# Expert weights of a mixture layer in 2 MB transfers of 16 KB rows, into pairs of slots

## Chip, cores, metric

One core of a Trainium2 chip runs the whole kernel. The metric is device time in microseconds (us) of one launch, lower is better.

## What is computed

One layer over 256 latent tokens and 256 context tokens of width 1024: a conditioned norm, one input projection, two attention branches (8 query heads over 2 key heads; 8 heads through low-rank projections), their gated sum, an output projection and a gated residual; then a second conditioned norm and a mixture of 32 experts, of which each token uses 4:

```python
x = x + g1 * y
x = x + g2 * _moe(_modulate(x, p['norm_ffn'], sh2, sc2), p)
# _moe, for each expert and its tokens xb:
gu = xb @ p['expert_w1'][eid] + p['expert_b1'][eid]      # 1024 x 2048
x_glu = jnp.minimum(gu[..., :1024], 7.0)
x_lin = jnp.clip(gu[..., 1024:], -7.0, 7.0)
act = x_glu * jax.nn.sigmoid(1.702 * x_glu) * (x_lin + 1)
y = act @ p['expert_w2'][eid] + p['expert_b2'][eid]      # 1024 x 1024
```

All of it is float32. The experts' weights are 32 x 12 MB, 384 MB (1 MB is 1,048,576 bytes; GB/s count 10^9 bytes).

## The kernel before

**The front** (the norm, projections, attention, output projection) is cut into named steps, generators whose every `yield` ends a piece. `PLAN`, a list of names written out at the top, says in which order the pieces are emitted (`mixer`); a step that needs another finishes that one first (`needs`). Weights of the front come through three buffers `w` of 1 MB, loaded by SyncE, which issues nearly all transfers, in one order. Products of the front split each operand into two float32r parts and multiply three times (`mm3`, L172 to L174). `reload` (step "x") folds the second norm's scale into the router weights `rw`; `out_chunk` adds the output projection to x, transposes x by 128 columns (`transpose`, L190) and multiplies by `rw` to get the router logits.

**The experts' weights** travel in 384 parts of 1 MB, 12 per expert: part i < 8 holds rows 128 i to 128 i + 127 of w1 (one 8 KB row per partition), parts 8 to 11 hold 256 rows of w2, two neighbouring rows (8 KB) per partition. `expert_part` takes the next slot of `RING`, 20 slots of 1 MB in fixed order (z0 z1, e0 to e3, n0 to n3, m0 m1, g0 g1, three w, y0 y1, r0), and issues the transfer (L105). A slot is a tile, so the transfer waits on SyncE until the readers of what lay there are done. Most slots serve the attention first. `ahead_of_time` fetches parts before the expert loop, by steps of the plan: EZ fetches 2 (z), EA 8 (e, n, when the attention's pools close), EG 4 (m, g). The other six slots come when the loop starts.

**Routing** (`route`) normalises x into `xn`, picks four experts per token, and numbers the tokens of each expert; an expert's first 64 tokens take part in the loop, and `overflow` handles the rest (it is skipped at run time where there are none).

**The expert loop** (`experts`, in an order kept by `keep_order`): for each pair of experts `gather` (L988) multiplies one-hot matrices with `xn` (xn is the loaded operand, 128 x 128) to fetch the tokens, transposed, and applies the second norm's scale and shift per column (`A2`, `B2`, eight columns of 128 features). `up` (L1013 biases, L1020 weights) accumulates 8 parts of w1. `swiglu` runs on VectorE and ScalarE. `turned` transposes the activations (L190, four transposes, every second element of a row of 256). `down` (L1054) accumulates 4 parts of w2, and `scatter` (L1069, L1070) adds the weighted rows to x. TensorE works on the gather of the next pair, or the scatter of the last, while `swiglu` runs. An expert with an even number scatters the pair before it, an odd one gathers for the next pair. Expert 2 also adds the second biases (`bias2`, L969).

Which feature lies in which partition is set by the slices of x and xn (128 features in a row) and by w1's rows; for w2 by `turned`.

Of the kernel before, what the change touches and what calls it, by code (L numbers as in the profile page):

```python
# [6 lines left out]
F32 = mybir.dt.float32  # L7
# [18 lines left out]
l3 h2 l4 k4 r4 r7 c0 EZ k5 c1 f7 k6 l2 h6 end T1 q0*4 q1 kv*2 ss q0 kv r6 q0 q1 kv q1*2 h5 l7 q1 q0 q1*2 g0 q0  # L26
kv q0 EZ mp rest*2 q1*2 q0 T1 g0 q0 g0 c7 g0 g1 c5 g0 c3 q1 g1 q1 g0*3 mp g1*2 g2 kv h7 S0 g2 EZ l6 P0 g0 g1*2
rest g2 g1*2 S2 mp P1 g2*3 g3 rest g2 g3 rest g1 rest S1 c4 S2 P2 l5 end g2 S0 rest S4 S6 rest V3 V2 S4 S3 P3
g3 rest g3*2 S5 S3 c6 g3*2 g2 P4 a0 g3 rest*2 a0 S6 g3 a0 rest a0*2 P5 rest*2 S5 rest V1 rest g2 S7 P6 rest*3
g3 S7 V6 a1 rest b0 k7 rest V0 a1*3 P7 S8 rest*2 a1 rest a0 V8 rest b1 V7 b1 b0 S1 b0 rest a2 P9 b0 V5 a0*2  # L30
rest a2 a1 a2*2 a1 b0 S10*2 V9 V4 a2 a3 b1 rest wa0 b0 b2 S8 V11 a3*4 a1 P13 a1 wa0 a3 a2*2 wa0 S12 rest*2 wa0
S12 rest b1 wa0 P8 wa0 b1 rest wa0 b2 P12 S11 S13 wa0 wa1 rest S9 S15 a3 P10 b2 wa1 wa0 a2 wa1 S9 a2 a3 S13
wa1*3 b3 a0 wa1 S11 b3 V12 V13 b2 S14*2 EA a3 wa1 wb0 b3 EA wb0 b2 P11 wb0 EA S15 wa1 wb0*3 rest wb0 EA wa1
wa0 wb1 b3 wb0*2 wb1 P14 b2 EA wb1 o0 late o0 wb1 rest wb1 o0 P15 wb1 late wb1 EA o0 wb1 o0*2 b1 o0 EA wb1
o1*2 wb1 late o0 o1*2 o0 EG*2 o1 o0*2 rest o1 V14 EG*2 V15 wb0 wb1 late wb0 o0 wb0 o1 late x EG V10 rest o1 b3
o1 EA wb1 late*3 EA b3 o1*3
"""
SLOTS = ("e0", "e1", "e2", "e3", "m0", "m1", "g0", "g1", "y0", "y1", "z0", "z1")
LATER = ("n0", "n1", "n2", "n3")

RING = ("z0", "z1", "e0", "e1", "e2", "e3") + LATER + ("m0", "m1", "g0", "g1") + ("w",) * NW + ("y0", "y1", "r0")

# [4 lines left out]

R_GQ, R_GK, R_MQ, R_MK, R_RB, R_N = 0, 128, 256, 448, 640, 672


class Layer:
# [9 lines left out]
    def open(self, ctx, name, bufs, **kw):  # L61
        self.n += 1
        kw.setdefault("reuse_waits", "tile")
        if name in ("ws", "r"):
            kw["side"] = "right"
        self.pools[name] = ctx.enter_context(self.tc.tile_pool(name=f"{name}{self.n}", bufs=bufs, **kw))
# [9 lines left out]
    def s(self, slot, shape, dt=F32):  # L76

        return self.tile("k" if slot == "x" else "s", shape, dt, slot, 1)

# [12 lines left out]

    def wx(self, shape, dt=F32):
        slot = RING[self.nx % len(RING)]
        self.nx += 1
        if slot == "w":
            return self.w(shape, dt)
        return self.tile({"n": "q", "r": "r"}.get(slot[0], "s"), shape, dt, slot, 1)
# [12 lines left out]
    def ahead_of_time(self, n):  # L111
        for _ in range(n):
            self.ahead.append(self.expert_part())
            yield

    def after_attention(self):
        self.attention.close()
        self.open(self.ctx, "q", 1)
        for slot in LATER:
            self.q([128, 2, D], slot, 1)  # L120
        self.q([128, D], "xg", 1)
        yield from self.ahead_of_time(8)

# [666 lines left out]
    def out_chunk(self, c):  # L790
# [7 lines left out]
        for t in range(2):  # L798
# [33 lines left out]
    def mixer(self):  # L832
# [7 lines left out]
        def gates(c):  # L840
            if c // 2 not in self.ga:
# [132 lines left out]
    def gather(self, e0):  # L974
# [139 lines left out]
    def overflow(self):  # L1114
# [6 lines left out]
        with tc.If(rv > 64):  # L1121
# [12 lines left out]
            with tc.For_i(0, NE, 1) as i:  # L1134
# [80 lines left out]
def pack(inputs):  # L1215
# [72 lines left out]
```

## Time and profile before

| | |
|---|---|
| median of 3 runs | 1319.28 us (1316.31 to 1319.49) |
| the profiled execution | 1318.76 us |
| its span, first to last instruction | 1317.0 us |
| mean granted TensorE clock in it | 0.978 |
| PE busy | 1220.3 us, 93% |
| weights' transfers (hardware queue) | 466.30 MB (10^6 bytes), 87.3% of 16 engines |
| expert transfers | 384 of 1 MB |

Times in rows are us from the first instruction, "x8" counts instructions, and L1020 is line 1020 of the kernel above. PE is TensorE's products, PEld its loading of the stationary operand, SPq SyncE's issuing of transfers. In rows of the chain a piece "DMA r<-in_w_dram" lasts from issue to landing.

### The profile page before, as it was taken

The page shows a single profiled execution, that of the slowest core. Times are in us where ns is not written, and L with a number is a line of the kernel's source. Part 1 is how long each engine was busy: PE and PEld are TensorE (multiplying, and loading weights), DVE is VectorE, ACT ScalarE, POOL GpSimd, SP SyncE. Part 2 cuts the span into 40 slices and gives each one's busy share as a digit, 9 for nine tenths or more (in the row PEclk, how much of TensorE's full clock was granted, in tenths as well). Part 3 has the DMA queues.
Part 4 walks back from the last instruction along what each step waited for, and adds up shares of the span by engine and source line. Part 5 has one row for each costly group of instructions (what it writes and reads, how often), then busy time and mean ns, then how long its engine had stood idle before and what let it go on. Part 6 is the DMA issues. An engine that isn't in the chain of part 4 may idle for free.

```text
span 1317.0 us, 15464 instructions
## 1 busy us (share of the span) xinstructions
PE 1220.3 (93%) x6143; PEld 594.7 (45%) x6143; DVE 475.4 (36%) x1037; ACT 289.3 (22%) x624; POOL 36.8 (3%) x84
## 2 busy tenths in 40 slices
PE   6999999899979999999999999999898998989896
PEld 4777776678744343333334333333323233333332
DVE  5578679876531312122221213222121221212122
ACT  2376778665420000001100001000000010000000
POOL 0220001000000000000000000000000000000000
PEclk8999999999989999999999999999999999999999
DMA  9834462258889999999999999999999999999995
GB/s 346 316 144 168 171 230 87 99 180 329 325 344 409 414 373 405 419 420 419 420 420 420 419 419 419 420 421 419 419 420 420 420 419 420 420 419 420 420 419 206
DMA packets 67324, 467.34 MB, mean 355 GB/s; under 512 B 7632, under 2 KB 8016, under 8 KB 11952
## 3 DMA queue, kind: packets, MB, share of 16 engines
q1 hardware_dynamic: 67248, 466.30, 87.3%
q8 instruction: 50, 0.82, 0.3%
q14 instruction: 26, 0.21, 0.0%
HBM read 465.23 MB, written 1.05 MB: 354 GB/s over the span
## 4 chain that ended last, share of the span: by engine, by line
PE 65%; DMA 27%; DVE 5%; ACT 2%; issue 1%; SPq 0%; POOL 0%; DVEq 0%; ACTq 0%; POOLq 0%
PE bs L1020 21%; PE bx L1054 11%; DMA r<-in_w_dram 8%; DMA m<-in_w_dram 6%; DMA n<-in_w_dram 5%; DMA e<-in_w_dram 5%; PE bacc L172 3%; PE bacc L173 3%; PE bacc L174 3%; DMA w<-in_w_dram 3%; PE bacc L988 2%; PE bx L277 2%; PE bx L190 2%; PE bacc L1069 2%; PE bt L988 2%; PE bt L1069 2%
## 5 line engine op out<-in xcount | busy, mean ns | idle before, releaser
L1028 DVE TENSOR_SCALAR a<-bs 128x512 f32<-128x512 f32 x32 | 22.1, 692 | 435.9 <-PE bs L1020 435.9
L1029 ACT ACTIVATE a<-a 128x512 f32<-128x512 f32 x32 | 20.1, 630 | 716.0 <-DVE a L1028 716.0
L1060 DVE TENSOR_TENSOR y<-bx,g 64x512 f32<-64x512 f32 x64 | 44.1, 689 | 212.3 <-PE bx L1054 211.6
L1020 PE MATMUL bs<-e,xg 128*64 128x512 f32 x416 | 94.2, 595 | 4.1 <-DMA e<-in_w_dram 4.1
L1020 PE MATMUL bs<-n,xg 128*64 128x512 f32 x400 | 90.8, 595 | 3.5 <-DMA n<-in_w_dram 3.5
L139 DVE TENSOR_TENSOR wl<-w,wh 128x512 fp32r<-128x512 f32 (+1 forms) x108 | 74.6, 696 | 30.1 <-ACT wh L138 29.4
L988 PE MATMUL bacc<-c,xn 128*128 128x128 f32 x256 | 42.1, 331 | 38.8 <-DVE c L981 38.8
L1020 PE MATMUL bs<-w,xg 128*64 128x512 f32 x312 | 72.2, 597 | 5.0 <-DMA w<-in_w_dram 4.9
L138 ACT CAST wh<-w 128x512 fp32r<-128x512 f32 (+1 forms) x108 | 65.4, 611 | 44.9 <-PE bacc L174 33.3
L988 PEld LDWEIGHTS bacc<-c,xn 128*128 128x128 f32 x256 | 38.3, 236 | 52.3 <-DVE c L981 51.0
L1020 PEld LDWEIGHTS bs<-e,xg 128*64 128x64 f32 x416 | 28.9, 137 | 67.1 <-issue 57.0
L1020 PEld LDWEIGHTS bs<-n,xg 128*64 128x64 f32 x400 | 27.7, 137 | 64.3 <-issue 56.4
L1020 PE MATMUL bs<-g,xg 128*64 128x512 f32 x208 | 47.7, 597 | 2.2 <-DMA g<-in_w_dram 2.2
L1054 PE MATMUL bx<-n,a 128*64 128x512 f32 x208 | 48.9, 613 | 0.7 <-ACT a L1042 0.7
L1020 PE MATMUL bs<-y,xg 128*64 128x512 f32 x208 | 47.4, 594 | 2.2 <-DMA y<-in_w_dram 2.2
L1020 PE MATMUL bs<-z,xg 128*64 128x512 f32 x208 | 47.5, 596 | 1.1 <-DMA z<-in_w_dram 1.1
L1054 PE MATMUL bx<-e,a 128*64 128x512 f32 x208 | 47.1, 595 | 0.0
L1020 PE MATMUL bs<-m,xg 128*64 128x512 f32 x192 | 44.0, 595 | 2.1 <-DMA m<-in_w_dram 2.1
L1020 PEld LDWEIGHTS bs<-w,xg 128*64 128x64 f32 x312 | 21.1, 136 | 53.9 <-issue 40.8
L998 POOL TENSOR_TENSOR c<-c,gm 128x128 f32<-128x128 f32 x32 | 12.1, 401 | 978.4 <-DVE c L981 854.8
L988 PE MATMUL bt<-c,xn 128*128 128x128 f32 x256 | 37.7, 296 | 0.0
L988 PEld LDWEIGHTS bt<-c,xn 128*128 128x128 f32 x256 | 35.5, 215 | 0.0
(360 smaller groups left out, 1949.8 us busy)
## 6 DMA issues: line engine op xcount, KB each, us to landing
e<-in_w_dram SPq DMA_DIRECT2D x78, 1024.0 KB, 19.9
n<-in_w_dram SPq DMA_DIRECT2D x76, 1024.0 KB, 19.9
w<-in_w_dram SPq DMA_DIRECT2D x57, 1024.0 KB, 19.9
z<-in_w_dram SPq DMA_DIRECT2D x40, 1024.0 KB, 19.9
m<-in_w_dram SPq DMA_DIRECT2D x38, 1024.0 KB, 19.9
g<-in_w_dram SPq DMA_DIRECT2D x38, 1024.0 KB, 19.9
y<-in_w_dram SPq DMA_DIRECT2D x38, 1024.0 KB, 19.9
w<-in_ada_dram SPq DMA_DIRECT2D x24, 1024.0 KB, 6.6
```

Of the source, the lines that this page charges most:

```text
L138: self.nc.scalar.copy(h, src)
L139: self.nc.vector.tensor_sub(l, src, h.bitcast(F32))
L172: mm(o, lh, rh, start=start, stop=False, **kw)
L173: mm(o, lh, rl, start=False, stop=False, **kw)
L174: mm(o, ll, rh, start=False, stop=stop, **kw)
L190: self.nc.tensor.transpose(o, i, self.ident)
L277: nc.tensor.matmul(b[j:j + 32, :256], c, u[:, kk], start=kk < 4, stop=kk >= 4, tile_position=(0, j))
L988: nc.tensor.matmul(b[:, kk % 2], self.xn[:, t, kk * 128:(kk + 1) * 128], oh[:, t], start=t == 0, stop=t == 1)
L1020: mm(b[64 * j:64 * j + 64], xg[:, k, e % 2], w[:, lo:lo + 512], start=False, stop=k == 7, tile_position=(0, 64 * j))
L1054: nc.tensor.matmul(b[64 * j:64 * j + 64], lh, w[:, i, j * 512:(j + 1) * 512], start=f == 0, stop=f == 7, tile_position=(0, 64 * j))
L1060: nc.vector.tensor_mul(y[r:r + 64, cs], b[q], self.g2[q, cs])
L1069: nc.tensor.matmul(b, G[r, t * 128:(t + 1) * 128], y[r, cs], start=True, stop=True)
```

## The change

**Transfers.** `RING` becomes nine pairs of slots (Z E F N O G M W Y, 2 MB each) and two single slots (V R), 20 MB as before. A transfer into a pair fetches two parts: of w1 256 rows, two neighbouring rows (16 KB) per partition; of w2 512 rows, four neighbouring rows (16 KB) per partition. `weights` hands out the halves one after the other. Single transfers of 1 MB fetch one half of such a unit (8 KB out of each 16 KB): in V and R, for parts 20 and 21, and for the last four parts. Pairs are persistent tiles, so a pair's transfer waits for both halves' readers.

**Order of features.** With two rows of w1 per partition, block k of 128 features holds every second feature of a group of 256. `rows(a, k)` takes these columns with step 2: in `gather`, in `out_chunk`'s transposes and in `normed_T` (overflow). The second norm's gains, shift and scale weights and the router weights are permuted alike on the host, in `pack`. `turned` transposes with step 4, and `down` takes one row block per part of `weights`.

**Space and plan.** e0 to e3 move to a pool of the attention; m, y and w buffers to pools that close before routing, behind which M, Y, W, V and R open. Ahead of the loop EZ fetches one pair, EA four (E F N O), EG one (G). `PLAN` is another list.

```diff
 PLAN = """
-f0 h0 f1 T0 bi T0 h1 T0 l0 l1 k0 f2 r1 T1 k1 r2 r0 c2 r3 T0*2 f3 k2 h3 f4 k3 T0 T1*2 h4 T1 T0 tab T1 r5 f5 f6
...
+r0 f0 h0 f1 T0 bi T0 h1 l1 k0 T0 l0 f2 T1 k1 c2 r3 T0*2 f3 k2 h3 f4 k3 h4 T1 tab r5 l3 r1 f6 h2 T0 f5 k4 r7 T1
...
 """
-RING = ("z0", "z1", "e0", "e1", "e2", "e3") + LATER + ("m0", "m1", "g0", "g1") + ("w",) * NW + ("y0", "y1", "r0")
+RING = "ZEFNOGMWYVR"
+def rows(a, k):
+
+    return a[:, k // 2 * 256 + k % 2:k // 2 * 256 + 256:2]
...
     def expert_part(self):
         e, i = divmod(self.nx, 12)
-        src = self.I["w1"][e, i * 128:i * 128 + 128] if i < 8 else self.I["w2"][e, i * 256 - 2048:i * 256 - 1792]
-        w = self.wx([128, 2 * D] if i < 8 else [128, 2, D])
-        self.nc.sync.dma_start(w, src if i < 8 else src.rearrange("(p j) d -> p j d", j=2))
-        return w
+        at = self.nx % sum(1 if slot in "VR" else 2 for slot in RING)
+        slot = "VR"[at - 18] if at >= 18 else RING[at // 2]
+        o = i % 2
+
+        size = 1 if slot in "VR" or 20 <= self.nx < 22 or self.nx >= 12 * NE - 4 else 2
+        self.nx += size
+        lo = 0 if slot in "VR" else at % 2 * 2 * D
+        ap = self.slots[slot][:, lo:lo + size * 2 * D]
+        if i < 8:
+            u = i // 2 * 256
+            src = self.I["w1"][e, u:u + 256].rearrange("(p j) f -> p j f", j=2)[:, o:o + size]
+            dst = ap.rearrange("p (j f) -> p j f", j=size)
+        else:
+            u = (i - 8) // 2 * 512
+            src = self.I["w2"][e, u:u + 512].rearrange("(p j) d -> p j d", j=4)[:, 2 * o:2 * o + 2 * size]
+            dst = ap.rearrange("p (j d) -> p j d", j=2 * size)
+        self.nc.sync.dma_start(dst, src)
+        return [dst[:, j] for j in range(dst.shape[1])]
     def weights(self):
-        return self.ahead.pop(0) if self.ahead else self.expert_part()
+        if not self.ahead:
+            self.ahead += self.expert_part()
+        return self.ahead.pop(0)
...
-                self.transpose(b[:, j], self.x[:, t, c * 512 + j * 128:c * 512 + (j + 1) * 128])
+                self.transpose(b[:, j], rows(self.x[:, t], 4 * c + j))
...
-        w.update(EZ=self.ahead_of_time(2), EA=self.after_attention(), EG=self.ahead_of_time(4))
+        w.update(EZ=self.ahead_of_time(1), EA=self.after_attention(), EG=self.ahead_of_time(1))
...
-                nc.tensor.matmul(b[:, kk % 2], self.xn[:, t, kk * 128:(kk + 1) * 128], oh[:, t], start=t == 0, stop=t == 1)
+                nc.tensor.matmul(b[:, kk % 2], rows(self.xn[:, t], kk), oh[:, t], start=t == 0, stop=t == 1)
...
-        pairs = act.rearrange("q (u p i) -> q u i p", u=2, i=2)
-        for c in range(4):
-            self.transpose(b[:, c], pairs[:, c // 2, c % 2])
+        rows = act.rearrange("q (p i) -> q i p", i=4)
+        for i in range(4):
+            self.transpose(b[:, i], rows[:, i])
...
-        for u in range(4):
+        for f in range(8):
             w = self.weights()
-            for i in range(2):
-                f = 2 * u + i
-                lh = aT[:, f % 4, u // 2 * 64:u // 2 * 64 + 64]
-                for j in range(2):
-                    nc.tensor.matmul(b[64 * j:64 * j + 64], lh, w[:, i, j * 512:(j + 1) * 512], start=f == 0, stop=f == 7,
-                                     tile_position=(0, 64 * j))
+            lh = aT[:, f % 4, f // 4 * 64:f // 4 * 64 + 64]
+            for j in range(2):
+                nc.tensor.matmul(b[64 * j:64 * j + 64], lh, w[:, j * 512:(j + 1) * 512], start=f == 0, stop=f == 7,
+                                 tile_position=(0, 64 * j))
...
+        for slot in "MYW":
+            self.slots[slot] = self.tile("r", [128, 4 * D], F32, slot, 1)
+        self.slots["V"] = self.tile("r", [128, 2 * D], F32, "V", 1)
+        self.slots["R"] = self.tile("r", [128, 2 * D], F32, "R", 1)
```

## Rows read from the trace of the kernel before

**Rows 1.** The page: span, slices of clock, DMA and rate, the chain's shares.
```profile
span 1317.0 us, 15464 instructions
...
PEclk8999999999989999999999999999999999999999
DMA  9834462258889999999999999999999999999995
GB/s 346 316 144 168 171 230 87 99 180 329 325 344 409 414 373 405 419 420 419 420 420 420 419 419 419 420 421 419 419 420 420 420 419 420 420 419 420 420 419 206
...
PE 65%; DMA 27%; DVE 5%; ACT 2%; issue 1%; SPq 0%; POOL 0%; DVEq 0%; ACTq 0%; POOLq 0%
```

**Rows 2.** Windows: length, busy PE PEld DVE ACT POOL (instructions), PEclk, DMA share, GB/s.
```profile
350.00:380.00 30.00, 26.17 (x167) 19.03 (x167) 15.07 (x52) 9.84 (x23) 0.76 (x2) 0.89 0.73 270
...
460.00:470.00 10.00, 10.00 (x44) 2.83 (x44) 2.64 (x4) 0.00 (x0) 0.00 (x0) 0.85 0.71 262
...
490.00:496.00 6.00, 6.00 (x37) 3.26 (x37) 0.73 (x2) 1.66 (x4) 0.00 (x0) 0.97 0.99 384
496.00:1297.00 801.00, 746.97 (x3566) 281.04 (x3562) 176.22 (x305) 58.09 (x120) 9.87 (x26) 0.99 1.01 419
```

**Rows 3.** The chain in order of time, whole run: start, us, piece.
```profile
830.53 1.02 PE bs L1013 x8
...
857.57 12.00 PE bs L1020 x55
869.58 19.89 DMA r<-in_w_dram
...
1271.63 19.90 DMA r<-in_w_dram
1291.57 1.94 PE bs L1020 x8
```

**Rows 4.** The chain over three experts, 570 to 692 us.
```profile
580.04 1.02 PE bs L1013 x8
581.05 13.91 PE bs L1020 x64
...
600.40 0.47 PE bx L190 x4
600.88 0.89 PE bt L988 x8
601.77 0.22 PE bx L190 x2
601.99 7.02 PE bx L1054 x32
609.01 1.02 PE bs L1013 x8
...
635.02 1.02 PE bs L1013 x8
```

**Rows 5.** DMA view: packets of 11 to 14 us, then of 500 to 1290 us.
```profile
DMA packets 338, 1.23 MB, mean 411 GB/s; under 512 B 37, under 2 KB 37, under 8 KB 338
...
DMA packets 45472, 331.43 MB, mean 420 GB/s; under 512 B 5045, under 2 KB 5045, under 8 KB 5045
```

**Rows 6.** SyncE's issues, 325 to 430 us and 476 to 500 us.
```profile
334.42 0.90 SPq L105 DMA_DIRECT2D m<-in_w_dram  x2
...
353.40 11.16 SPq L105 DMA_DIRECT2D w<-in_w_dram  x3
...
366.27 0.44 SPq L105 DMA_DIRECT2D r<-in_w_dram  x1
378.68 2.04 SPq L105 DMA_DIRECT2D z<-in_w_dram  x2
...
481.69 14.29 SPq L105 DMA_DIRECT2D e<-in_w_dram  x4
```

**Rows 7.** All engines, 488 to 502 us, about the restart.
```profile
491.95 3.65 PE L1054 MATMUL bx<-e,a 128*64 128x512 f32 x16
...
493.93 2.04 SPq L105 DMA_DIRECT2D e<-in_w_dram  x2
```

**Rows 8.** Windows, sum of 0 to 377 us.
```profile
sum 377.00, PE 351.67 PEld 265.85 DVE 266.69 ACT 220.47 POOL 25.45; mean PE 70.33 PEld 53.17 DVE 53.34 ACT 44.09 POOL 5.09
```

More of the change, by code (lines that the diff above doesn't have):

```diff
@@ L24 @@
 PLAN = """
-f0 h0 f1 T0 bi T0 h1 T0 l0 l1 k0 f2 r1 T1 k1 r2 r0 c2 r3 T0*2 f3 k2 h3 f4 k3 T0 T1*2 h4 T1 T0 tab T1 r5 f5 f6
[L26 to L34, printed above, removed]
@@ L35 @@
-o1*2 wb1 late o0 o1*2 o0 EG*2 o1 o0*2 rest o1 V14 EG*2 V15 wb0 wb1 late wb0 o0 wb0 o1 late x EG V10 rest o1 b3
-o1 EA wb1 late*3 EA b3 o1*3
-"""
-SLOTS = ("e0", "e1", "e2", "e3", "m0", "m1", "g0", "g1", "y0", "y1", "z0", "z1")
-LATER = ("n0", "n1", "n2", "n3")
-RING = ("z0", "z1", "e0", "e1", "e2", "e3") + LATER + ("m0", "m1", "g0", "g1") + ("w",) * NW + ("y0", "y1", "r0")
+r0 f0 h0 f1 T0 bi T0 h1 l1 k0 T0 l0 f2 T1 k1 c2 r3 T0*2 f3 k2 h3 f4 k3 h4 T1 tab r5 l3 r1 f6 h2 T0 f5 k4 r7 T1
+c0 T0 EZ T1 r4 k5 c1 l4 f7 k6 h6 end T1*2 q0*5 q1 kv*2 r6 T1 ss q0 q1 kv q1 r2 q1 c7 q0 q1*3 q0 kv l2 mp q0 EZ
@@ new lines @@
+g0 rest kv rest q1 q0 g0 q0 c5 h5 l7 q1 g0*3 q1 g0 g1 q1 g1 c3 g0 g1 mp g0 g2 EZ g1 kv h7 S0*2 g2 S2 l6 P0
+g1*3 g2*2 g1 mp S2 g2*2 P1 rest g2 S4 rest S6 g2 rest g0 g3 rest g3 l5 g1 rest c4 P2 end rest P3 rest V3 S4
+g3*2 S3 g3 V2 S1 g3 S5 c6 g3 g2*2 g3 rest P4 a0 rest a0 S6 a0 rest a0 rest g3 a0 P5 rest g3 rest S5 rest*2 V1
+S3 rest S7 P6 V0 rest S7 V6 a1 P7 rest b0 k7 a1 rest S8 a1 rest*2 a1 rest a1 V8 b1*2 rest b0 a0 a2 a0 V7 P9 a1
+a2 V5 a0 a2 rest b0 a2 S10 S1 b0 S10 b0 V9 b0 V4 b1 wa0 b2 a2 a1 a2 a3*4 V11 a3 P12 rest wa0 P8 a2 a1 S8 a3
@@ new lines @@
+wa0 a2 P13 wa0 S13 S12 rest wa0 S11 wa0 S12 wa0 rest*2 wa0 b2 b1 S9 S15 a3 rest b3 P10 a3 wa1 wa0 wb1 wb0 a2
+wa1 wa0 S11 a3 wa1 b2 wa1 S14 V13 S13 wa1 b2 b3 EA*2 wa1*2 S14 wa1 b3 b1 b3 wb0 b2 wb0 EA S15 wb0 P11 wb0 S9
+wb0 wa1 rest wb0 wa1 o0 late o0 wb0 o0 wb1 o0*2 EA*2 wb1 rest V12 wb1 o0 P14 P15 b2 rest a1 EA wb1 o1 wb0
+wb1*2 EA wb1 a0 wb1 o0 o1 EG b1 o0*2 EG o1 x V15 o1 o0 o1 o0 V10 late b3 o1 V14 EG late o1 wb0 wb1 wb0 o1 rest
+wb0 o0 wb1 rest o1*2 late EG o1 rest late wb1 EA EG late*2 o1 late b3 EA
@@ L63, in open @@
         kw.setdefault("reuse_waits", "tile")
-        if name in ("ws", "r"):
+        if name in ("ws", "r", "ym", "w"):
             kw["side"] = "right"
@@ L76, in s @@
     def s(self, slot, shape, dt=F32):
-        return self.tile("k" if slot == "x" else "s", shape, dt, slot, 1)
+        if slot[0] == "g":
+            return self.slots["G"][:, int(slot[1]) * 2 * D:int(slot[1]) * 2 * D + 2 * D].rearrange("p (t d) -> p t d", t=2)
+        return self.tile({"x": "k", "e": "e"}.get(slot[0], "ym"), shape, dt, slot, 1)
     def h(self, tag, shape, dt=F32):
@@ L91, in q @@
         return self.tile("q", shape, dt, tag, bufs)
[L93 to L98, printed above, removed]
     def expert_part(self):
         e, i = divmod(self.nx, 12)
-        src = self.I["w1"][e, i * 128:i * 128 + 128] if i < 8 else self.I["w2"][e, i * 256 - 2048:i * 256 - 1792]
-        w = self.wx([128, 2 * D] if i < 8 else [128, 2, D])
-        self.nc.sync.dma_start(w, src if i < 8 else src.rearrange("(p j) d -> p j d", j=2))
-        return w
+        at = self.nx % sum(1 if slot in "VR" else 2 for slot in RING)
[15 more added lines that the diff above has]
+        return [dst[:, j] for j in range(dst.shape[1])]
     def weights(self):
-        return self.ahead.pop(0) if self.ahead else self.expert_part()
+        if not self.ahead:
+            self.ahead += self.expert_part()
+        return self.ahead.pop(0)
     def ahead_of_time(self, n):
         for _ in range(n):
-            self.ahead.append(self.expert_part())
+            self.ahead += self.expert_part()
             yield
@@ L118, in after_attention @@
         self.open(self.ctx, "q", 1)
-        for slot in LATER:
-            self.q([128, 2, D], slot, 1)
+        for slot in "EFNO":
+            self.slots[slot] = self.q([128, 4 * D], slot, 1)
         self.q([128, D], "xg", 1)
-        yield from self.ahead_of_time(8)
+        yield from self.ahead_of_time(4)
     def k(self, shape, tag, dt=F32):
@@ L939, in normed_T @@
                 for t in range(2):
-                    self.transpose(b[:, j, t * 128:(t + 1) * 128], self.xn[:, t, (kk + j) * 128:(kk + j + 1) * 128])
+                    self.transpose(b[:, j, t * 128:(t + 1) * 128], rows(self.xn[:, t], kk + j))
             for j in range(2):
@@ L1139, in overflow @@
                 v.tensor_scalar_add(ctr, ctr, 1.0)
-                w1 = I["w1"][bass.ds(i, 1)].rearrange("o (k p) f -> p (o k) f", p=128)
+                w1 = I["w1"][bass.ds(i, 1)].rearrange("o (u p j) f -> p (o u) j f", p=128, j=2)
                 w2 = I["w2"][bass.ds(i, 1)].rearrange("o (k p) d -> p (o k) d", p=128)
                 for c in range(4):
-                    wg, wl, wd = self.wx([128, 8, 256]), self.wx([128, 8, 256]), self.wx([128, 2, D])
+                    wg, wl = (self.slots["ZEFY"[c]][:, j * 2 * D:(j + 1) * 2 * D].rearrange("p (k f) -> p k f", k=8)
+                              for j in range(2))
+                    wd = self.slots["MMGG"[c]][:, c % 2 * 2 * D:(c % 2 + 1) * 2 * D].rearrange("p (j d) -> p j d", j=2)
                     b1 = self.a([1, 2, 256])
                     lo = c * 256
-                    nc.sync.dma_start(wg, w1[:, :, lo:lo + 256])
-                    nc.sync.dma_start(wl, w1[:, :, D + lo:D + lo + 256])
+                    for u in range(4):
+                        nc.sync.dma_start(wg[:, 2 * u:2 * u + 2], w1[:, u, :, lo:lo + 256])
+                        nc.sync.dma_start(wl[:, 2 * u:2 * u + 2], w1[:, u, :, D + lo:D + lo + 256])
                     nc.sync.dma_start(wd, w2[:, 2 * c:2 * c + 2])
@@ L1194, in build @@
         self.loaded, self.ahead, self.nsplit, self.nx = {}, [], 0, 0
-        self.open(self.ctx, "w", 1)
+        self.slots = {}
+        self.attention = ExitStack()
         self.open(self.ctx, "s", 1)
-        for slot in SLOTS:
-            self.s(slot, [128, 2, D])
-        self.attention = ExitStack()
+        for slot in "ZG":
+            self.slots[slot] = self.tile("s", [128, 4 * D], F32, slot, 1)
+        self.open(self.attention, "e", 1)
+        for j in range(4):
+            self.s(f"e{j}", [128, 2, D])
         with ExitStack() as pre:
+            self.open(pre, "ym", 1)
+            for slot in ("y0", "y1", "m0", "m1"):
+                self.s(slot, [128, 2, D])
+            self.open(pre, "w", 1)
             self.open(pre, "ws", 1)
@@ L1220, in pack @@
     o = {"x": g["x"][0], "ctx": g["ctx"][0]}
+    perm = np.arange(D).reshape(4, 128, 2).transpose(0, 2, 1).reshape(-1)
     ab = g["ada_b"][0].reshape(6, D)
     o["cols"] = np.concatenate(
-        [col(g["norm_mix"][0]), col(g["norm_ffn"][0]), col(ab[0]), col(ab[1]), col(ab[3]), col(ab[4]),
+        [col(g["norm_mix"][0]), col(g["norm_ffn"][0][perm]), col(ab[0]), col(ab[1]), col(ab[3][perm]), col(ab[4][perm]),
          np.stack([g["c"][0], g["c_ctx"]], -1).reshape(8, 128, 2).transpose(1, 0, 2).reshape(128, 16),
@@ L1228, in pack @@
     o["gb"] = np.stack([ab[2], ab[5]])
-    aw = g["ada_w"][0].reshape(8, 128, 6, D).transpose(2, 1, 0, 3)
+    aw = g["ada_w"][0].reshape(8, 128, 6, D).transpose(2, 1, 0, 3).copy()
     units = []
     for sh, sc, gg in ((0, 1, 2), (3, 4, 5)):
+        if sh:
+            aw[3:5] = aw[3:5][..., perm]
         for i in range(8):
```

2 lines of the change are left out of this document (1 added, 1 removed).

## The prediction

> **What bounds the kernel now.** I read the page's slices first. The DMA row fills up at about a third of the span and stays at 9 to the end, with 420 GB/s in nearly every slice, while the chain gives PE 65% and DMA 27% [rows 1]. So two stages of different kind share the expert loop, and the windows and the chain in order of time tell where one gives way to the other. From 496 us to 1297 us the DMA share is 1.01 [rows 2]. Yet in the expert loop the long pieces of the chain are PE's until 869.58 us, and transfers stand in it only behind that [rows 3]. The reader should see a tank: two experts cost PE 635.02 - 580.04 = 54.98 us [rows 4], and their 24 MB cost DMA 24 x 1.0486 / 420 = 59.92 us [rows 5]. DMA is the slower of the two, but it starts 20 slots ahead, so PE needs until 870 us to drink the lead. The end is therefore set by DMA: the moment when DMA last stood still, plus the bytes left at the rate of DMA, plus a tail of 1317.0 - 1291.57 = 25.4 us [rows 1, 3]. DMA last falls short in 490 to 496 us (384 GB/s, share 0.99); earlier it falls short at 350 to 380 us and at 460 to 470 us, always because all slots are full [rows 2]. The restart is visible: SyncE issues four transfers into e over 14.29 us, two of them at 493.93 us [rows 6, 7], 2.0 us behind the first product of expert 3's w2, which frees a part every 7.02 / 4 = 1.75 us [rows 4]. That transfer is part 64 of 384, so 320 parts remain, 320 x 2.497 us = 799 us of the 823 us that are left.
>
> The profiled execution took 1318.76 us, 0.5 us under the median of 1319.28 us. 0.3% is 4.0 us, about what a measurement of this kernel can tell from no change.
>
> **The change part by part.** *Longer rows.* A 1 MB transfer of 128 rows of 8 KB becomes 2 MB of 128 rows of 16 KB, at the same number of bytes. The trace has no 16 KB row in a weight queue, so I bound it from shorter ones. In 11 to 14 us only rows of 4 KB move (1.23 MB in 301 packets besides the small ones) at 411 GB/s; rows of 8 KB move at 420 GB/s [rows 5]. With 16 engines, a 4 KB row takes 16 x 4096 / 411 = 159.5 ns of an engine and an 8 KB row 16 x 8192 / 420 = 312.1 ns: 152.6 ns for each further 4 KB, and 6.9 ns that each row pays once. A 16 KB row is then 312.1 + 2 x 152.6 = 617.3 ns where two of 8 KB take 624.2 ns: 1.1% less, 424.7 GB/s. Of the 320 parts left at the restart, 284 go in pairs; slots V and R (32 parts) and the last four stay single with rows of 8 KB. Gain: 284 x 2.497 x 1.1% = 7.8 us. The ends: no gain at all if the row costs twice what 8 KB cost, and 1.9%, 13 us, if the short window is read 1.5% too fast. A loss I can't exclude: rows of 16 KB, and single halves that skip every second 8 KB, read memory in another order. I allow 4 us for that, half the gain. I take 7.8 us, since both rows that I extrapolate from move at full share.
>
> The Trainium skill, "DMA: Bandwidth & Descriptors", section Bandwidth (why small descriptors are slow), gives a packet about 3 cycles beside its beats of 32 bytes. By that a 16 KB row would take 515 cycles where two of 8 KB take 518, an estimate of 0.6% and 4 us; the two rates measured here would have to lie closer together for that.
>
> *Pairs of slots.* A transfer into a pair waits for both halves. While the ring is full this delays DMA by one part's use: 1.75 us at the restart. Earlier delays vanish in the wait for PE, and later there are none, for the lead only falls from then on (59.9 against 55.0 us). What is queued behind the waiting transfer on SyncE is only the next weights. Sum: +1.7 us. Where PE has caught up, behind 870 us, PE now gets two parts at once and idles longer between; that costs nothing, because the last w1 parts (V, R) and the last four are single, so the tail keeps its shape.
>
> *Strided reads on TensorE.* The 32 weight loads of each gather, one gather per two experts, now step over every second element; the 4 transposes per expert in `turned` step by 4 where they stepped by 2; 16 transposes in `out_chunk` step by 2. Four transposes with step 2 take 0.47 us in the chain, two with step 1 0.22 us, and eight gather products 0.89 us: 0.118 against 0.110 us each, so 0.0075 us for step 2 [rows 4]. Before the restart lie three gathers (96 loads), 16 loads in `turned` at an assumed 0.015 us more, and the 16 in `out_chunk`: 0.7 + 0.2 + 0.1 = 1.0 us, all on PE's chain, hence on the end. Ends: 0, and 14 us if each strided load took twice as long. Behind the restart, 0.4 us per two experts hides in the 4 us by which DMA's pace is slower than PE's, and the tail has one `turned`, below 0.1 us.
>
> *Fetching ahead.* Before, 14 parts are issued ahead of routing, m and g at 334 to 336 us among them [rows 6]; now 12, for M, Y, W, V and R open only when the attention's space closes. M's 2 MB (5.0 us) move behind about 353 us. DMA has 27% of 30 us free in 350 to 380 us, 8 us [rows 2], and the old ring issued its last slot at 366.27 us and then stood until 378.68 us [rows 6]. So 5 us fit: 0. If that cover were gone the price would be 5 us.
>
> *Order.* The list of steps is another one, with the same steps in number for PE. Up to 377 us PE is busy for 351.67 us [rows 8], so a better order can win less than 25 us, and PE mostly has work whatever the order. Nothing in the trace of before tells a sign; I take 0, with 8 us to either side, a third of that idle time. In it lies that each pair in the attention stands on SyncE ahead of weights of that stage: 2.5 us more in the queue each, over four pairs 10 us if nothing covered it.
>
> Sum: 1318.76 - 7.8 + 1.7 + 1.0 + 0 = 1313.7 us.
>
> **The rivals.**
> *Rows are cut.* If a 16 KB row goes out as two packets of 8 KB, or costs twice one of 8 KB, the gain is nothing and the costs stay: 1318.76 + 1.7 + 1.0 = 1321.5 us. For it: no 16 KB packet of weights has been seen here. Against it: rows of 4 KB and 8 KB already differ by 2% [rows 5]. The Trainium skill, same page, section Specifications, has line rate from 512 B on, which speaks for this rival; the two rates here speak against it.
>
> *PE becomes the bound, slower.* Place: gathers and `turned`, 40 strided loads per two experts. Without waits for DMA, PE would have reached the end of expert 31's w1 products at 830.53 (expert 16) + 7 x 54.98 + 26 + 14.9 = 1256.3 us; it reached it at 1293.5 us [rows 3, 4]. So PE holds 37 us, 2.3 us for each of 16 pairs, 0.058 us per load: from there on it decides. If each load took 0.11 us more (twice), 4.4 us per pair, the end is 1317.0 - 37 + 16 x 4.4, with 1.8 us around the span: 1352 us. Step 2 at 0.118 us speaks against it; step 4 is not shown in this trace. The Trainium skill, "SBUF — State Buffer", in its note on 16-byte lines, wants two reads per line for full rate: step 2 in fp32 has two, step 4 one. By that only `turned`, 8 loads per pair, would pay, and twice its time is 0.9 us per pair, under the limit.
>
> *The order of the front decides.* 8 us earlier, 1305.7 us, or 8 us later, 1321.7 us and more. For it: the new list is long and differs nearly from its first word. Against: PE is full for most of that stage.
>
> **How the numbers follow.** Chances: forecast 0.55; rows cut 0.15; PE the bound 0.08; front earlier 0.11, later 0.11. The forecast's own spread (0 to 13 us of gain, costs from 1 us up) leaves it faster by over 0.3% (below 1315.3 us) in 0.44 of its 0.55, else within. Rows cut: 0.02 faster, 0.10 same, 0.03 slower. PE the bound: 0.02 same, 0.06 slower. Front earlier: 0.11 faster; later: 0.02 same, 0.09 slower. Together 0.57, 0.25, 0.18. The range goes from 1313.7 less 5 us more gain and 8 us of front, 1301 us, to rows cut with a front 5 to 6 us later, 1327 us; PE as the bound and a worse front lie outside.
>
> **What would show it.** Right: packets of 16 KB; 425 GB/s in the windows behind 500 us; a first transfer in the chain later than 870 us; gather products at 0.118 us; first expert near 376 us. Wrong: 420 GB/s and packets of 8 KB (rows cut); no transfers in the chain behind 900 us (PE the bound); the first expert's bias product away from 375.75 us by more than 5 us (the front).

## The result and the profile after

The changed kernel took 1306.88 us, median of 4 runs (1305.55 to 1307.49), beside 1318.39 us for the kernel before (4 runs, 1316.31 to 1319.49). The ratio is 0.9913, 95% interval 0.9896 to 0.993: 0.9% faster, 11.5 us. The profiled execution took 1305.55 us with a span of 1303.8 us. The forecast was 1313.7 us, a gain of 5.1 us; the direction and the place of the gain came out as forecast, its size was twice as large.

The page after: span, slices, packets, and the chain's shares, which answer to [rows 1].

```profile
span 1303.8 us, 15107 instructions
...
GB/s 349 313 149 164 206 207 89 97 98 354 295 377 417 421 397 410 426 425 427 425 426 428 425 425 426 426 425 427 426 425 427 426 425 428 425 424 429 426 424 197
...
PE 69%; DMA 21%; DVE 6%; ACT 2%; issue 1%; SPq 0%; POOL 0%; DVEq 0%; ACTq 0%
...
E<-in_w_dram SPq DMA_DIRECT2D x19, 2048.0 KB, 33.7
```

The slices that stood at 419 to 421 GB/s now stand at 424 to 429. DMA has lost 6 points of the chain, and 4 of them went to PE. The same in the DMA view of 500 to 1280 us:

```profile
DMA packets 25295, 332.25 MB, mean 426 GB/s; under 512 B 2809, under 2 KB 2809, under 8 KB 2809
```

For about the same bytes there were 45472 packets at 420 GB/s [rows 5]. Without the 2809 small ones a packet now has 332.25 MB / 22486 = 14776 bytes on average, more than the 8192 of an old row. So the rows do go out whole, and the queue moves 1.4% more. The windows after, with the columns of [rows 2]:

```profile
350.00:380.00 30.00, 25.47 (x158) 17.03 (x159) 12.50 (x48) 7.52 (x19) 0.76 (x2) 0.89 0.82 317
460.00:470.00 10.00, 10.00 (x52) 3.02 (x50) 1.38 (x2) 0.00 (x0) 0.00 (x0) 1.00 0.83 326
490.00:496.00 6.00, 6.00 (x30) 1.87 (x26) 0.00 (x0) 0.00 (x0) 0.00 (x0) 1.00 0.97 341
496.00:1284.00 788.00, 740.76 (x3555) 284.90 (x3554) 176.66 (x306) 57.88 (x120) 9.87 (x26) 0.99 1.01 425
```

DMA still falls short last at 490 to 496 us, a little more than before (341 GB/s against 384). The stretch 350 to 380 us took up the fetches that had moved there: its share rose from 0.73 to 0.82 [rows 2]. Now the chain over the whole run, which answers to [rows 3]:

```profile
968.16 3.53 PE bs L1036 x15
971.70 34.33 DMA O<-in_w_dram
...
1234.67 38.22 DMA Y<-in_w_dram
1272.93 7.09 PE bs L1036 x32
1280.02 1.91 PE bacc L1083 x4
```

The first long transfer in it stands at 971.70 us instead of 869.58. A faster queue should empty its lead later, and the prediction named this as a sign; but it is a weak one. Run 3 below has the same rate, and its first transfer stands at 848.85 us; run 10, at the same rate too, has it at 864.12 us. At the end the last pair that PE waits for, Y, lands at 1272.93 us, and PE then needs 7.09 us for four parts; V and R, the two single parts behind Y, came in under that. Expert 31's w1 products end at 1280.02 us; before, they ended at 1293.51 us [rows 3]. So 13.5 us were won up to there and nothing behind it: 1303.8 - 1280.02 = 23.8 us remain, against 23.5 us.

The chain over two experts, which answers to [rows 4]:

```profile
577.60 1.02 PE bs L1029 x8
578.61 13.91 PE bs L1036 x64
...
595.01 2.15 PE bacc L1004 x16
597.17 0.94 PE bt L1004 x8
598.11 0.47 PE bx L206 x4
...
632.78 1.02 PE bs L1029 x8
```

632.78 - 577.60 = 55.18 us, 0.20 us more than before. Eight gather products with step 2 take 0.94 us (0.89 before); the four transposes of `turned`, with step 4 now, take the same 0.47 us as with step 2. Last, SyncE's issues around the restart, and the bias product of expert 4 from the chain, which answer to [rows 6, 7]:

```profile
480.64 0.33 SPq L118 DMA_DIRECT2D E<-in_w_dram  x1
493.00 0.33 SPq L118 DMA_DIRECT2D F<-in_w_dram  x1
496.44 0.33 SPq L118 DMA_DIRECT2D N<-in_w_dram  x1
```
```profile
496.39 1.02 PE bs L1029 x8
```

Pair F is parts 64 and 65. It goes out 3.39 us ahead of expert 4's bias product; two single transfers into those slots went out 5.11 us ahead of it (run 1 below, its issue and its bias product):

```profile
491.65 2.04 SPq L118 DMA_DIRECT2D F<-in_w_dram  x2
```
```profile
496.76 1.02 PE bs L1029 x8
```

The difference, 1.72 us, is the pair's wait for its second half.

### The profile page after: what moved, and what is told of

Read it like the earlier page. It is cut to its first block, busy times and chain, and to the rows that moved or that the text cites. A ratio compares the mean times of both kernels' runs of the same rounds, so it can differ in the third digit from the quotient of the medians.

```text
span 1303.8 us, 15107 instructions
## 1 busy us (share of the span) xinstructions
PE 1212.9 (93%) x6143; PEld 596.6 (46%) x6143; DVE 472.7 (36%) x1037; ACT 287.7 (22%) x624; POOL 34.9 (3%) x84
## 4 chain that ended last, share of the span: by engine, by line
PE 69%; DMA 21%; DVE 6%; ACT 2%; issue 1%; SPq 0%; POOL 0%; DVEq 0%; ACTq 0%
PE bs L1036 25%; PE bx L1068 13%; DMA W<-in_w_dram 3%; PE bacc L188 3%; DMA Y<-in_w_dram 3%; PE bacc L189 3%; PE bacc L190 3%; PE bacc L1004 3%; DMA E<-in_w_dram 3%; DMA R<-in_w_dram 3%; DMA G<-in_w_dram 3%; DMA F<-in_w_dram 3%; DMA O<-in_w_dram 3%; PE bt L1004 2%; PE bx L293 2%; PE bx L206 2%
## 5 line engine op out<-in xcount | busy, mean ns | idle before, releaser
L1036 PE MATMUL bs<-E,xg 128*64 128x512 f32 x208 | 46.9, 593 | 2.7 <-DMA E<-in_w_dram 2.7
L1036 PE MATMUL bs<-Y,xg 128*64 128x512 f32 x208 | 47.2, 596 | 2.1 <-DMA Y<-in_w_dram 2.1
L1036 PE MATMUL bs<-Z,xg 128*64 128x512 f32 x208 | 47.3, 596 | 1.7 <-DMA Z<-in_w_dram 1.7
L1036 PE MATMUL bs<-N,xg 128*64 128x512 f32 x208 | 46.9, 593 | 1.8 <-DMA N<-in_w_dram 1.8
L1036 PE MATMUL bs<-M,xg 128*64 128x512 f32 x208 | 47.2, 596 | 1.3 <-DMA M<-in_w_dram 1.3
L1036 PE MATMUL bs<-W,xg 128*64 128x512 f32 x208 | 46.9, 593 | 1.2 <-DMA W<-in_w_dram 1.2
L1036 PE MATMUL bs<-F,xg 128*64 128x512 f32 x208 | 47.2, 596 | 0.5 <-DMA F<-in_w_dram 0.5
L1036 PE MATMUL bs<-G,xg 128*64 128x512 f32 x192 | 43.4, 594 | 1.8 <-DMA G<-in_w_dram 1.6
L1036 PE MATMUL bs<-O,xg 128*64 128x512 f32 x192 | 43.6, 596 | 1.2 <-DMA O<-in_w_dram 1.2
L1029 PE MATMUL bs<-b,ck 32*64 32x512 f32 x256 | 34.8, 612 | 0.0
```

Source lines behind the costliest of these rows:

```text
L1029: mm(b[64 * j:64 * j + 64], self.ck[r, K_E32 + e:K_E32 + e + 1].broadcast_to([32, 64]), self.b12[r, j * 512:j * 512 + 512], start=True, st ...
L1036: mm(b[64 * j:64 * j + 64], xg[:, k, e % 2], w[:, lo:lo + 512], start=False, stop=k == 7, tile_position=(0, 64 * j))
```

## The experiments

My theory (L) after the result: the gain is the length of the rows alone, since each row pays a fixed time, and the lead that the slots give sets when it shows. Rivals: the size and number of the transfers (T), the reordered front (P), and, for what limits the change from here, the strided weight loads on TensorE. Each kernel is the changed one with an edit, unless another is named.

**1. Every transfer single: 1 MB in rows of 8 KB.** The pairs of slots, the row order and the plan stay.

```diff
-        size = 1 if slot in "VR" or 20 <= self.nx < 22 or self.nx >= 12 * NE - 4 else 2
+        size = 1
...
-            self.ahead += self.expert_part()
+            self.ahead += self.expert_part() + self.expert_part()
```


> The changed kernel with every transfer cut to one half: 1 MB, 128 rows of 8 KB, each row 16 KB behind the one before; slots, plan, order of features and steps as in the changed kernel. Theory L (a row pays a fixed time, so longer rows move faster): rate back to 419 to 421 GB/s behind 500 us, packets of 8 KB only, 1316 to 1321 us (13 us of rate back, less 1.7 us since no transfer waits for a second half). Theory T (fewer, larger transfers do it): also slower, by the same 11 us, so this run alone does not part L from T. Theory P (the new plan does it): 1306 to 1308 us. If skipping every second 8 KB in memory costs by itself, the rate is below 418 GB/s.

Measured: 1318.11 us (10 runs) beside 1319.57 us, ratio 0.9989 (0.9979 to 0.9999). The DMA view of 500 to 1280 us:

```profile
DMA packets 44903, 327.27 MB, mean 420 GB/s; under 512 B 4983, under 2 KB 4983, under 8 KB 4983
```

The old rate is back, and with it nearly the old time, although each transfer now reads 8 KB out of every 16 KB. So skipping 8 KB in memory costs nothing here, and all else in the change (order of features, strided loads, plan, pools) is worth under 3 us in sum (0.9979 x 1319.57 is 2.8 us less). A sum can hide parts that cancel: run 3 finds one.

**2. 2 MB transfers of rows of 8 KB.** Pairs as in the change, but of 256 short rows, in the old order of features.

```diff
-            src = self.I["w1"][e, u:u + 256].rearrange("(p j) f -> p j f", j=2)[:, o:o + size]
+            src = self.I["w1"][e, u:u + 256].rearrange("(j p) f -> p j f", j=2)[:, o:o + size]
...
-            src = self.I["w2"][e, u:u + 512].rearrange("(p j) d -> p j d", j=4)[:, 2 * o:2 * o + 2 * size]
-            dst = ap.rearrange("p (j d) -> p j d", j=2 * size)
+            src = self.I["w2"][e, u:u + 512].rearrange("(h p j) d -> p h (j d)", h=2, j=2)[:, o:o + size]
+            dst = ap.rearrange("p (h x) -> p h x", h=size)
```


> The changed kernel with its 2 MB transfers made of 256 rows of 8 KB (the order of features of the kernel before, so gathers with step 1 and turned with step 2 again). Theory L: 8 KB packets, 420 to 421 GB/s behind 500 us, 1318 to 1321 us. Theory T: 425 GB/s or more, 1305 to 1308 us. On TensorE eight gather products take 0.89 us in the chain again, against 0.94 us in the changed kernel.

Measured: 1318.55 us (10 runs), ratio 0.9991 (0.9981 to 1.0002).

```profile
DMA packets 42698, 327.56 MB, mean 420 GB/s; under 512 B 2741, under 2 KB 2741, under 8 KB 2741
```

Half the transfers, the same rate. T falls; with run 1, L is what is left of the theories named for the rate.

**3. The old plan in the new kernel.**

```diff
 PLAN = """
-r0 f0 h0 f1 T0 bi T0 h1 l1 k0 T0 l0 f2 T1 k1 c2 r3 T0*2 f3 k2 h3 f4 k3 h4 T1 tab r5 l3 r1 f6 h2 T0 f5 k4 r7 T1
...
+f0 h0 f1 T0 bi T0 h1 T0 l0 l1 k0 f2 r1 T1 k1 r2 r0 c2 r3 T0*2 f3 k2 h3 f4 k3 T0 T1*2 h4 T1 T0 tab T1 r5 f5 f6
...
```


> The changed kernel with the list of steps of the kernel before. Theory L: the first expert's bias product within 3 us of 375.6 us, 425 GB/s, total 1304 to 1310 us. Theory P: 5 us or more slower than the changed kernel, and the first expert begins later by as much.

Measured: 1316.61 us (10 runs), ratio 0.9986 (0.9973 to 0.9998), though the steady rate is 426 GB/s as in the changed kernel:

```profile
DMA packets 25087, 332.27 MB, mean 426 GB/s; under 512 B 2782, under 2 KB 2782, under 8 KB 2782
```

SyncE's issues and the chain say where the gain went:

```profile
304.02 0.33 SPq L118 DMA_DIRECT2D E<-in_w_dram  x1
...
305.34 0.62 SPq L118 DMA_DIRECT2D O<-in_w_dram  x1
308.38 0.33 SPq L510 DMA_DIRECT2D w<-in_wout_dram  x1
...
369.05 0.33 SPq L118 DMA_DIRECT2D M<-in_w_dram  x1
```
```profile
308.38 21.79 DMA w<-in_wout_dram
...
382.46 1.02 PE bs L1029 x8
```

Four pairs, 8 MB, go out in a row, and the attention's next weights stand behind them for 21.79 us, in the chain. The first expert's bias product comes at 382.46 instead of 375.58 us, 6.9 us later, and the stretch 350 to 380 us is used to 0.46 instead of 0.82. The expectation for L missed, and what theory P expected of this run came true: L holds for the rate, but most of the gain in time depends on the plan. By the medians it is 9.7 us (1316.61 against 1306.88). The profiled execution of run 3, at 1312.12 us the fastest of its ten, is 6.6 us behind that of the changed kernel, and the 6.9 us of the front account for it; where the medians' further 3 us lie, no trace shows. The plan of the changed kernel sends E, F and N at 295.76 to 296.66 us and O and G only at 322.32 and 329.23 us, with four loads of `wout` before, between and behind those two.

**4. The new plan alone, in the kernel before.** The inverse of run 3's edit, on the other kernel.

> The kernel before with the list of steps of the changed kernel. Theory L: 420 GB/s and within 4 us of the kernel before, 1315 to 1322 us. Theory P: faster than the kernel before by 5 us or more.

Measured: 1317.52 us (10 runs), ratio 0.9983 (0.9972 to 0.9993). So the plan by itself gives about 2 us by the medians, at the old rate (419 GB/s). The trace doesn't show where: the first expert comes 2.5 us later than in the kernel before, not earlier.

```profile
378.29 1.02 PE bs L1013 x8
```

Runs 3 and 4 together: neither plan nor rows do it alone; the plan's worth lies in the room it makes for pairs.

**5. Rows of 4 KB.** Each transfer goes out as two, each with half of every row.

```diff
-        self.nc.sync.dma_start(dst, src)
+        for h in range(2):
+            self.nc.sync.dma_start(dst[:, h], src[:, h])
```


> The changed kernel with rows of 4 KB: each transfer split in two, of the two half rows of w1 (or of two of four rows of w2), so 1 MB and 256 packets of 4 KB per transfer; slots, plan and TensorE's work as in the changed kernel. It measures the short end of theory L over 790 us instead of 3 us. With a fixed time per row of 10.3 ns, which the 8 KB and 16 KB rows give together (312.1 and 613.9 ns): 161.2 ns per row, 406 to 407 GB/s, 1343 to 1348 us. With the prediction's 6.9 ns: 159.5 ns, 411 GB/s, 1334 to 1338 us. If the row length plays no part below 16 KB: 420 GB/s, 1318 us.

Measured: 1341.26 us (4 runs) beside 1318.98 us, ratio 1.0166 (1.0149 to 1.0183).

```profile
DMA packets 83105, 318.92 MB, mean 409 GB/s; under 512 B 5338, under 2 KB 5338, under 8 KB 83069
```

The series is now 409, 420 and, where nearly all rows are 16 KB (run 7), 427 GB/s. By 16 engines a row takes 16 x 4096 / 409 = 160.2 ns, 312.1 ns and 16 x 16384 / 427 = 613.9 ns. Doubling the row saves 2 x 160.2 - 312.1 = 8.3 ns the first time and 2 x 312.1 - 613.9 = 10.3 ns the second. The time fell between the two ranges expected for a constant of 6.9 and of 10.3 ns, so neither constant fits.

**6. A tenth pair in place of V and R; single transfers only at the restart and at the end.** It removes the pair's wait at 493 us and the 32 short-rowed parts.

```diff
-RING = "ZEFNOGMWYVR"
+RING = "ZEFNOGMWYV"
...
-        size = 1 if slot in "VR" or 20 <= self.nx < 22 or self.nx >= 12 * NE - 4 else 2
+        size = 1 if 20 <= self.nx < 22 or 64 <= self.nx < 66 or self.nx >= 12 * NE - 6 else 2
```


> The changed kernel with V and R joined to a tenth pair (so no 8 KB rows but for the last six parts), and with parts 64 and 65, whose transfer restarts DMA behind the gather of expert 4, sent singly. Theory: the end is the restart plus bytes at DMA's rate. 32 parts at 16 KB instead of 8 KB rows: 1.4 us less; restart one part's use earlier: 1.7 us less. 427 GB/s, 1302 to 1305.5 us. If the end is not set that way, 1306 to 1308 us.

Measured: 1305.02 us (4 runs), ratio 0.9895 (0.9878 to 0.9912). Parts 64 and 65 go out 5.11 us ahead of expert 4's bias product, so the wait is gone; in time that is 1.9 us under the changed kernel, where 3.1 us were expected, and inside both intervals, so the time doesn't show that the wait's end is worth anything.

**7. 18 slots instead of 20.** V and R are left out; all but 8 parts go in pairs.

```diff
-RING = "ZEFNOGMWYVR"
+RING = "ZEFNOGMWY"
...
-        size = 1 if slot in "VR" or 20 <= self.nx < 22 or self.nx >= 12 * NE - 4 else 2
+        size = 1 if 18 <= self.nx < 20 or self.nx >= 12 * NE - 6 else 2
```


> The changed kernel without slots V and R: nine pairs, 18 slots, all rows 16 KB but for parts 18, 19 and the last six. By the theory of the lead (all slots full at the restart, then DMA alone sets the end) two slots fewer cost 2 x 2.456 = 4.9 us, and 32 parts with longer rows win 1.4 us back: 1309 to 1312 us, and the first transfer in the chain comes earlier than in the changed kernel (971.7 us), by about 70 us. If the slots' number plays no part: 1304 to 1306 us.

Measured: 1309.25 us (4 runs), ratio 0.9928 (0.9912 to 0.9945). The DMA view of 500 to 1280 us, and the first long transfer in the expert loop's chain:

```profile
DMA packets 23065, 332.82 MB, mean 427 GB/s; under 512 B 2564, under 2 KB 2564, under 8 KB 2564
```
```profile
890.98 34.63 DMA Z<-in_w_dram
```

The queue is as fast as in the changed kernel and in run 6 (426 GB/s both). Beside the changed kernel the 2.4 us lie inside the intervals. Run 6, with 20 slots, nearly all rows of 16 KB and the same runs to compare with, is the better partner: its four runs (to 1307.19 us) all lie under the four of run 7 (from 1308.89), the medians are 4.2 us apart, and expert 31's w1 products end at 1279.45 against 1283.95 us. That is the tank of the prediction, with two parts less in it. In size it fits only roughly: two parts are 4.9 us, and the pair's wait at the restart, which run 6 lacks, is another 1.7. The moment at which the lead is empty (891 against 972 us, and 942 in run 6) fits, but it scatters too much between kernels of 20 slots to show it (864 in run 10).

**8. w1 in 4 MB transfers of 32 KB rows.** Four rows of w1 per partition, so a block of 128 features has step 4, and `gather` loads it so.

```diff
-    return a[:, k // 2 * 256 + k % 2:k // 2 * 256 + 256:2]
+    return a[:, k // 4 * 512 + k % 4:k // 4 * 512 + 512:4]
...
+        if 20 <= self.nx < 22 or 64 <= self.nx < 66 or self.nx >= 12 * NE - 6:
+            size = 1
+        elif i >= 8 or self.nx < 22 or 64 <= self.nx < 68 or self.nx >= 12 * NE - 8:
+            size = 2
+        else:
+            size = 4
```


> Five quads of slots in place of pairs: w1 in transfers of 4 MB with rows of 32 KB (from part 24 on), w2 in 2 MB as in the changed kernel, gathers with step 4, parts 64 and 65 single. Theory L with 10.3 ns per row: 32 KB in 1217.6 ns, 430.6 GB/s for w1, 429 GB/s in all, 4 to 5 us less than with pairs alone: 1297 to 1303 us, if the front is not later. If the gain ends at 16 KB: 427 GB/s, 1302 to 1307 us. Eight gather products with step 4 take 0.94 us if step 4 costs what step 2 does, 1.0 us or more if it costs extra. If the quads' waits hold up the front, the first expert begins later than 375.6 us by as much as is lost.

Measured: 1336.44 us (4 runs), ratio 1.0134 (1.0117 to 1.0151). The chain over two experts:

```profile
588.50 1.02 PE bs L1031 x8
...
605.92 4.00 PE bacc L1006 x16
609.92 1.87 PE bt L1006 x8
611.79 0.47 PE bx L208 x4
612.25 1.85 PE bt L1006 x8
...
647.36 1.02 PE bs L1031 x8
```

Two experts cost PE 58.86 us instead of 55.18, and the gather has all of it: (4.00 - 2.15) + (1.87 - 0.94) + (1.85 - 0.94) = 3.69 us over 32 products, 0.115 us each. No transfer stands in the chain of the expert loop any more: PE is the bound. The longer rows can't show. Both ranges of the expectation missed; of its branches, the extra cost of step 4 came true.

**9. 32 KB rows again, with plain gathers.** `xn` is written once in the new order, so the gather's loads have step 1; quads from part 132 on.

```diff
-            nc.scalar.activation(self.xn[:, t], self.x[:, t], AF.Copy, scale=rstd[:, t:t + 1])
+            u = dict(j=4, p=128)
+            nc.scalar.activation(self.xn[:, t].rearrange("q (u j p) -> q u p j", **u), self.x[:, t].rearrange("q (u p j) -> q u p j", **u),
+                                 AF.Copy, scale=rstd[:, t:t + 1])
...
-                nc.tensor.matmul(b[:, kk % 2], rows(self.xn[:, t], kk), oh[:, t], start=t == 0, stop=t == 1)
+                nc.tensor.matmul(b[:, kk % 2], self.xn[:, t, kk * 128:(kk + 1) * 128], oh[:, t], start=t == 0, stop=t == 1)
```


> The quads of the run before (rows of 32 KB for w1), but from part 132 on only, and with the normalised tokens written once in permuted order, so that the gathers load with step 1. If the loss of the quads was the gathers' step 4 on TensorE, eight gather products take 0.89 us again, two experts 55.0 us, transfers stand in the chain again behind some 970 us, and with 32 KB rows at 430.6 GB/s for w1 the rate behind part 132 is 428 to 430 GB/s: 1299 to 1304 us. If the quads' coarse waits were the loss: slower than the pairs, above 1308 us, with a DMA share below 1 behind 600 us. If the gain of row length ends at 16 KB: 427 GB/s and 1303 to 1306 us.

Measured: 1305.67 us (4 runs) beside 1320.34 us, ratio 0.9895 (0.9878 to 0.9911). The DMA view of 700 to 1250 us:

```profile
DMA packets 10845, 236.13 MB, mean 429 GB/s; under 512 B 1208, under 2 KB 1208, under 8 KB 1208
```

Eight gather products are at 0.89 us and the rate rose as forecast, but the time is that of run 6: the expectation missed. Expert 31's w1 products end at 1278.68 us, 1.3 us ahead of the changed kernel. The chain shows why the rate did not become time. Its last long transfer lands at 1214.86 us:

```profile
1177.07 37.79 DMA H<-in_w_dram
1214.90 8.81 PE bs L1040 x32
```

Behind it everything up to 1278.68 us is PE's work on experts 29 to 31 and no transfer; in run 6 PE still waits for a pair and goes on only at 1272.37 us. So at the end the transfers are ahead again, and PE's pace behind its last wait sets the time. That this wait is so long because a piece is now up to four parts fits, but was not tried by itself.

**10. Run 6 with plain gathers.** As in run 9, with pairs (`j=2`).

> The kernel with ten pairs and parts 64 and 65 single, with the normalised tokens written in permuted order, so gathers load with step 1. Theory: step 2 cost the gathers 0.0065 us per load, 0.2 us per two experts, nearly all of it hidden behind DMA: 0 to 1 us less than 1305.0 us, eight gather products in 0.89 us, and 2 ScalarE writes of 128 x 1024 with a step, once, at most 1 us longer on the way to the first gather.

Measured: 1306.07 us (4 runs), ratio 0.989 (0.9874 to 0.9907), against run 6's 0.9895. The 0 to 1 us less that were expected did not come, within the noise. Gather loads with step 2 cost nothing that shows where DMA is the bound. Of the versions, run 6 has the lowest median, but runs 6, 9, 10 and the changed kernel can't be told apart.

## Why the prediction came out as it did

**What bounds the kernel: right.** The end follows the last restart of DMA, the bytes left and DMA's rate. Runs 1, 2 and 5 changed the rate and little else, run 7 the lead, run 8 PE's pace, and each moved the end to the side that the tank says. The moment at which the first transfer enters the chain is the weak part of the picture: it scatters by 100 us and more at one rate (848.85 us in run 3, 971.70 in the changed kernel).

**Longer rows: the step that was mis-sized.** The prediction put 6.9 ns of fixed time on a row, so 617.3 ns for 16 KB, 424.7 GB/s and 7.8 us. From the restart to the landing of part 377 the kernel before took 1291.57 - 2 x 2.50 - 493.93 = 792.6 us [rows 3, 7]; the changed one took 1272.93 - 493.00 = 779.9 us. That is 12.7 us over 314 parts, 284 of them in pairs: 1.8% each, near the 613.9 ns against 624.2 ns of the full series (1.65%). Two things made the step too small. The 411 GB/s for 4 KB rows came from 3 us with 338 packets [rows 5]; over 780 us, run 5 has 409, and the fixed time is 8.3 ns. And it is not quite a constant: the next doubling saved 10.3 ns. Why, no run shows; half as many transfers for the same rows (run 2) change the rate by only 0.1% (327.56 against 327.27 MB in 780 us). The upper end given, 13 us, stood for a short window read 1.5% too fast; it was 0.5%, and the rest is the second doubling. That end did hold the measured term. The lower end, a loss through reading memory in another order, is excluded by run 1.

The Trainium skill, "DMA: Bandwidth & Descriptors", section Bandwidth (why small descriptors are slow), led to an estimate of 0.6% and 4 us; the traces have about three times that. Its section Specifications, line rate from 512 B, doesn't hold here to the last percents: between 4 and 16 KB rows the rate rose by 4.4%.

**Pairs of slots: right to the number.** 1.7 us forecast, 1.72 us measured at the restart, and run 6 takes the wait away; its price in the time is below what the runs can tell.

**Strided reads: the loads right, `turned` wrong, the sum not found.** Step 2 costs the gather's loads (0.94 - 0.89) / 8 = 0.006 us each, as forecast (0.0075). `turned` with step 4 was given 0.015 us per transpose and costs nothing over step 2 (0.47 us for four in either). So two experts cost 0.20 us more, where the prediction allowed 0.4. From expert 0's bias product to expert 4's, run 4 (no strided gathers) takes 498.79 - 378.29 = 120.50 us and the changed kernel 120.81. Run 10 can't find the 1.0 us in the time.

**Fetching ahead: right.** M went out at 357.06 us and the stretch 350 to 380 us had the room; expert 0's bias product came at 375.58 us, before at 375.75.

**Order: right as a number, for a reason that only runs 3 and 4 show.** It was put at 0 with 8 us to either side. The front did end where it had (0.2 us earlier), but as the sum of two effects. With the old plan the pairs put it 6.7 us later (382.46 us, run 3) by standing ahead of the attention's weights on SyncE, the mechanism that the prediction named at up to 10 us. The new plan takes 6.9 us off that, though in the kernel before it adds 2.5 us (run 4). That the two cancel was luck: the prediction had no reason for it.

**The sum.** At the end of expert 31's w1 products: -12.7 (rate) + 1.7 (pair) - 2.6 (expert 4 is reached at 496.39 instead of 499.04 us) = -13.6, measured -13.5. All terms are read from the same two traces, so the sum has to close; it tells where the time lies. The 2.6 us don't belong to the change: the lead arises between 404 and 470 us with the granted clock, whose shares are means over 1.2 and 2.4 GHz (0.85 [rows 2] against 1.00 in 460 to 470 us). In the kernel before, PE paused at 416 to 424 us (busy 5.49 of 8 us) and the clock stood at 0.76 and 0.81 in the 8 us from 420 on; in the changed kernel PE paused as long (5.48 us busy) and the clock stayed at 1.00. Which of the two comes is not tied to the change: over 404 to 440 us run 2, which has the new plan, shows the 0.95 of the kernel before, and run 4, on the kernel before, shows the changed kernel's 1.00:

```profile
404.00:440.00 36.00, 33.48 (x174) 14.62 (x168) 6.98 (x14) 3.09 (x7) 0.76 (x2) 0.95 1.01 412
404.00:440.00 36.00, 33.48 (x176) 13.62 (x174) 6.84 (x14) 3.10 (x7) 0.76 (x2) 1.00 1.01 421
404.00:440.00 36.00, 33.48 (x170) 14.63 (x168) 6.22 (x13) 3.09 (x7) 0.76 (x2) 0.95 1.01 413
404.00:440.00 36.00, 33.48 (x180) 13.23 (x178) 7.38 (x14) 3.09 (x7) 0.76 (x2) 1.00 1.01 420
```

The rows are the kernel before, the changed one, run 2 and run 4. From expert 0's bias product to expert 4's the first and the third take 123.3 and 123.1 us, the second and the fourth 120.8 and 120.5. So of the 8.2 us by which the profiled execution of the changed kernel came under the forecast, 4.9 are the mis-sized row term (12.7 against 7.8), and 2.6 are luck with the clock.

**The rivals.** Rows are cut: fallen by the packets and the rate. PE as the bound: it didn't come about in the change, but run 8 shows it as described. Its threshold was 0.058 us per strided load over 40 loads, 2.3 us for two experts; step 4 brought 3.7 us, and the prediction's formula with it gives 1317.0 - 37 + 16 x 3.69 + 1.8 = 1340.8 us, where 1336.44 us were measured. The place was the gather, not `turned`.

## What to carry to other kernels

Where a stage stands at a full DMA share, rows of 16 KB instead of 8 KB still won 1.7% of the transfer time; the size of the transfer (1 or 2 MB, run 2) and gaps of 8 KB between rows (run 1) made no difference. Read a rate for such a step from a window of hundreds of microseconds: half a percent of error in it moved the fixed time of a row from 8.3 to 6.9 ns. And when transfers get coarser, look first at what stands behind them on the same queue: here 6.6 us (profiled executions) to 9.7 us (medians) of the gain hung on sending them between, not ahead of, the loads of the stage that runs.

## What the runs showed of the hardware beyond that

A gather product, whose loaded operand is 128 x 128 in fp32, costs 0.111 us with columns at step 1, 0.118 us at step 2 and 0.233 us at step 4 (0.89, 0.94 and 1.87 us for eight): step 2 is nearly free, step 4 doubles the time. The records of the loads alone, which overlap, point the same way (217, 219 and 328 ns on average for the `bt` half of the gathers between 560 and 760 us, in the kernel before, the changed one and run 8). The Trainium skill, "SBUF — State Buffer", in its note on 16-byte lines, wants two accesses per line for full rate, which fp32 has at step 2 and not at step 4; the gather's loads agree, while four transposes in `turned` take 0.47 us with either step, which the note doesn't tell apart. Why the transposes are spared was not tried.
